# Sums of squares of k, q and the outputs made in parts, inside a two-layer decoder trunk

## The chip, the core and the metric

The kernel runs on one core of a Trainium2 chip, in one launch. The metric is the device time of one execution in microseconds (us); lower is better. TensorE is PE below (its weight loads PEld), VectorE is DVE, ScalarE is ACT, GpSimd is POOL, and SyncE, which issues most weight loads, is SP.

## What is computed

A causal decoder trunk of two layers for 512 tokens of width 1024, in float32. Each layer is a mixer, a cross attention into 256 memory tokens and a gated convolutional feed-forward net. The change lies in the mixer of layer 0, and there in its gated delta rule: 4 heads of 128, with k and q normalised to length 1 and the output normalised again per head.

```python
qkv = silu(causal_dwconv(qkv, conv_qkv))
q, k, v = heads(qkv)                       # 4 heads x 128
q, k = l2_normalize(q), l2_normalize(k)    # x * rsqrt(sum(x * x) + 1e-6)
beta, g = sigmoid(b), -exp(a_log) * softplus(a + dt_bias)
o = gated_delta_rule_chunked(q, k, v, g, beta)     # q is scaled by 128 ** -0.5 inside
o = rms_norm(o, onorm_g) * silu(gate)
y_b = glu(gelu(s5_ssm(u)))                 # a diagonal state-space model beside it
x = x + concat(o, y_b) @ w_out
```

So three sums of squares are needed for each token and head: of k, of q, and of the output o.

## The kernel before

Activations lie transposed: 128 features on the partitions, 512 tokens along the free dimension. A float32 product is made of three matmuls (`mm3`, L182 to L187), with each operand split into a rounded part (`wh`, `xh`) and a rest (`wl`, `xl`). Weights come by DMA into three `raw` tiles; ACT rounds them (`wh`, L136) and DVE subtracts (`wl`, L141), for some of them POOL adds the rest by an accumulating DMA (L139). A sum over the 128 features of a head is a matmul of a tile of squares with a column of ones: `sumsq` (L764) makes one column for each head and chunk of 128 tokens, 4 per tile, each of them two records in the trace.

The mixer is a list of steps, `MIX`, at the head of the file. It is the order in which the program is written. PE and SP run in exactly that order; DVE, ACT and POOL run in an order that a scheduler makes when the program is built, so a change to one step can move other instructions on them.

The steps that matter here:

- `k`, `kc`, `qp` project k and q, convolve them (`cv`, L753 to L756), and square them on ACT (L761). `ba` makes beta and the decay g; its exponential and logarithm (L690 to L722) work on DVE in columns of `area`, a PSUM tile of 1024 columns that `column` (L107) hands out slice by slice.
- `ssk` (L863) is k's sums: 16 columns into a PSUM tile called `tr`, one of a ring of six (`psum`, L116), then 1 / sqrt on DVE (`rsqrt`, L197, some ten short instructions L204 to L211).
- `gc`, `rg`, `eg`, `rk` sum g up and lay the factors out as rows: `rows3` (L283) splits 32 columns into three parts on DVE (`R`, L290 to L293), transposes them on PE (L295), and ACT rounds the result (`RT`, L297). `dec` then multiplies them out into rows on PE (`row`, L305 and L307).
- `su` (`ssm_u`, L1377) brings u of the state-space model into another layout through DRAM: DVE scales (`sp`, L1383), ACT's queue stores (`du`, L1385) and loads it in four parts (`su`, L1388).
- `qk` (L934) makes the masked scores and q's sums; `B` is one piece of the memory's keys (`kp`) and values (`vp`), used to fill PE; `xa`, `xb` (`xstage`, L1011) and `ya`, `yb` (`ystage`) are steps of the inverse of a triangular matrix.
- `cs` updates the state, `co` (L1072) makes the outputs of one chunk in PSUM (`po`) and copies them into `oT` on ACT; `so` (L1085) squares the four `oT`, sums them in 16 columns, and makes from q's and the output's sums the factor `ro`, which `rr` and `yo` use.

The memory's norm (`r`, made by the same `rsqrt`) is laid out as rows by `row` (L262) for `B`.

Of the kernel before, what the change touches and what calls it, by code (L numbers as in the profile page):

```python
# [21 lines left out]
D = 1024  # L22
# [6 lines left out]
EPS = 1e-6  # L29
# [16 lines left out]
k3 k0 ba rs k1 rb kc1 bt su0 k2 kc2 su3 kc3 kc0 qp3 ssk sw0 gc su1 vp1 rg eg rk dec0 dec1 kh1 sw1 vp3 dec3 kh2 st0  # L46
dec2 am1 kh0 su2 am2 am0 kh3 sc0 vt3 am3 i i i i vp0 i st1 vp2 i i i i i i i sc1 sy0 gp1 i i gp3 i i i i sw2 qp1 vt1 i
gp2 qp2 i i qp0 i vt2 gp0 i i i i i sy1 ea0 i i i ea1 i i qk1 st2 ea2 i qk0 eb2 i i i ea3 mem kt2 qk3 qk2 B ya0 ya1
sc2 eb3 eb1 ya2 eb0 ya3 B sw3 B xa0 xa1 xa3 vt0 yb0 B xa2 yb2 B kt0 xb0 yb3 xb2 kt1 B W2 yb1 sy2 U2 B U0 B xb3 W0 xb1
kt3 U3 U1 W1 cs0 co0 W3 B cw1 B cs1 B B B co1 B B B cw2 st3 cs2 cw3 sc3 B co2 co3 B so B ld sy3 B B rr B B B B gu0 yo2  # L50
B gu1 B B yo0 B yo1 B yo3 B B gu2 gu3
# [5 lines left out]
class Net:  # L57
# [49 lines left out]
    def column(self, n, s="y"):  # L107

        if self.area is None:
            return self.tiny(n, s)  # L110
        if self.cur + n > 1024:
            self.cur = 0
        self.cur += n
        return self.area[:, self.cur - n : self.cur]
# [649 lines left out]
    def sumsq(self, squares):  # L764

        ps = self.psum("tr")
        for h, sq in enumerate(squares):
            for c in range(4):
                self.nc.tensor.matmul(ps[:, h * 4 + c : h * 4 + c + 1], sq[:, c * 128 : (c + 1) * 128], self.ones[:, 0:1], start=True, stop=True)  # L769
        return ps[:, : 4 * len(squares)]  # L770

    def mixer0(self, N, kv_out, x):
# [26 lines left out]
        g, ro = mp(16, "g"), mp(16, "ro")  # L799
# [62 lines left out]

        def ssk():  # L863
            va = self.tiny(16, "ssk")
            v.tensor_scalar(va, self.sumsq(sqk), EPS, None, ALU.add)
            self.rsqrt(va, 16, out=rkG[:, 0:16])
# [67 lines left out]
        def qk(h):  # L934
            ps = self.psum("qk")
            for c in range(4):
                nc.tensor.matmul(ps[:, CS[c]], kT[h][:, CS[c]], qT[h][:, CS[c]], start=True, stop=True)
            a = decT[h]
            v.tensor_tensor(a, ps, a, ALU.mult)
            QK[h] = a  # L940
            sq = ssq[:, 4 * h : 4 * h + 4]
            v.tensor_scalar(sq, self.sumsq([sqq[h]]), EPS, None, ALU.add)
            ps = self.rowr(D["Rk"], range(16 + 4 * h, 20 + 4 * h))
            v.tensor_tensor(qT[h], qT[h], ps, ALU.mult)
# [199 lines left out]
        def ld():  # L1144
# [5 lines left out]
            k=k, kc=kc, rs=rs, rb=rb, ba=ba_, bt=bt_, vp=vp, gp=gp, qp=qp, ssk=ssk, gc=gc, rg=rg, eg=eg, rk=rk, dec=dec, kh=khat, am=amat,  # L1150
# [440 lines left out]
```

## Time and profile before

| | us |
|---|---|
| median of 3 runs (lowest to highest) | 1418.5 (1417.56 to 1419.75) |
| the profiled execution | 1423.21 |
| its span, first to last instruction | 1421.2 |
| PE busy in the span | 1362.0 |
| DVE, ACT, POOL busy in the span | 915.4, 623.5, 222.6 |
| mean granted clock of TensorE | 0.970 of full |

The span is that of the profiled execution, whose own time is 2.0 us longer than its span and 4.7 us longer than the median. An engine's busy time says how much it has to do; what bounds the kernel at a place is read from the idle time of the engine that is busy nearly always, PE, and from what ended that idle time. A granted clock of 1 stands for 2.4 GHz and of 0.5 for 1.2 GHz.

### The profile page before, as it was taken

The numbers are of one execution on the slowest core, as the hardware profiler recorded it, in microseconds if no ns is written. First come the engines' busy times: TensorE is split into PE (matmuls) and PEld (weight loads), VectorE is DVE, ScalarE is ACT, GpSimd is POOL, SyncE is SP. The second block draws the span as 40 slices with busy tenths as digits, with TensorE's granted clock in tenths as the row PEclk, the third lists the DMA queues.
The fourth block names the chain that finished last, engine by engine and source line by source line (L and its number), as shares of the span: only waits on it lengthen the run. The fifth ranks groups of instructions, "written<-read, shape, count | busy, mean of one in ns | idle before, by whom it ended". The sixth has DMA issues, their size and how long they took to land.

```text
span 1421.2 us, 17648 instructions
## 1 busy us (share of the span) xinstructions
PE 1362.0 (96%) x6699; PEld 1150.6 (81%) x6699; DVE 915.4 (64%) x1551; ACT 623.5 (44%) x951; POOL 222.6 (16%) x351
## 2 busy tenths in 40 slices
PE   8599987999999999999999999989999999999997
PEld 6578876987788888888888888768888888888886
DVE  7867968457655567637754765975657746763764
ACT  6347564545434444314432445554444413431442
POOL 2594826220200200000000002210110000000003
PEclk9779968999999999999999999999999999999998
DMA  7343524375331233233333235942233333323221
GB/s 226 101 99 80 149 48 109 87 189 140 104 89 46 87 91 95 84 113 95 104 89 104 90 97 153 227 116 59 65 100 96 97 100 94 103 75 119 86 68 69
DMA packets 50772, 147.16 MB, mean 104 GB/s; under 512 B 7680, under 2 KB 13952, under 8 KB 50688
## 3 DMA queue, kind: packets, MB, share of 16 engines
q1 hardware_dynamic: 40480, 127.29, 29.4%
q0 software_dynamic: 3888, 14.16, 5.8%
q10 hardware_dynamic: 6320, 4.60, 1.1%
q8 instruction: 52, 0.85, 0.2%
q14 instruction: 32, 0.26, 0.1%
HBM read 141.83 MB, written 4.19 MB: 103 GB/s over the span
## 4 chain that ended last, share of the span: by engine, by line
PE 79%; DMA 3%; DVE 2%; ACT 2%; issue 1%; POOL 1%; ACTq 0%; POOLq 0%; SPq 0%
PE in L185 13%; PE in L187 13%; PE in L186 13%; PE op L186 9%; PE op L185 9%; PE op L187 9%; DMA raw<-in_wk 1%; PE kp L187 1%; PE kp L186 1%; PE kp L185 1%; DMA wl<-in_wk 1%; PE tr L769 1%; PE vp L185 1%; PE vp L186 1%; PE sc L187 1%
## 5 line engine op out<-in xcount | busy, mean ns | idle before, releaser
L136 ACT CAST wh<-raw 128x1024 fp32r<-128x1024 f32 (+1 forms) x230 | 237.4, 1036 | 397.6 <-PE op L186 152.0
L185 PE MATMUL in<-xh,wh 128*128 128x512 f32 x992 | 392.0, 395 | 13.2 <-DVE vl L374 6.3
L186 PE MATMUL in<-xl,wh 128*128 128x512 f32 x992 | 389.7, 393 | 0.0
L187 PE MATMUL in<-xh,wl 128*128 128x512 f32 x992 | 389.0, 392 | 0.0
L141 DVE TENSOR_TENSOR wl<-raw,wh 128x1024 fp32r<-128x1024 f32 (+1 forms) x203 | 244.1, 1205 | 79.4 <-ACT wh L136 77.1
L185 PEld LDWEIGHTS in<-xh,wh 128*128 128x128 f32 x992 | 188.5, 190 | 52.3 <-DVE vl L374 6.5
L187 PEld LDWEIGHTS in<-xh,wl 128*128 128x128 f32 x992 | 188.3, 190 | 39.6
L186 PEld LDWEIGHTS in<-xl,wh 128*128 128x128 f32 x992 | 188.4, 190 | 39.2 <-DVE xl L227 0.9
L247 POOL TENSOR_TENSOR sq<-sq,sq 128x512 f32<-128x512 f32 x28 | 47.5, 1698 | 973.2 <-ACT sq L242 875.2
L469 DVE TENSOR_TENSOR x<-op,x 128x512 f32<-128x512 f32 x68 | 46.9, 691 | 151.7 <-PE op L187 151.7
L185 PE MATMUL op<-fh,wh 128*128 128x512 f32 (+1 forms) x376 | 141.4, 376 | 0.0
L187 PE MATMUL op<-fh,wl 128*128 128x512 f32 (+1 forms) x376 | 141.2, 375 | 0.0
L186 PE MATMUL op<-fl,wh 128*128 128x512 f32 (+1 forms) x376 | 141.2, 375 | 0.0
L572 DVE TENSOR_TENSOR h<-in,rB 128x512 f32<-128x512 f32 x88 | 60.2, 688 | 87.1 <-PE in L187 87.1
L186 PEld LDWEIGHTS op<-fl,wh 128*128 128x128 f32 x376 | 70.8, 188 | 12.8
L185 PEld LDWEIGHTS op<-fh,wh 128*128 128x128 f32 x376 | 70.8, 188 | 12.8
L187 PEld LDWEIGHTS op<-fh,wl 128*128 128x128 f32 x376 | 70.8, 188 | 12.8
L192 ACT CAST fh<-a 128x512 fp32r<-128x512 f32 x44 | 27.3, 621 | 110.6 <-DVE a L584 110.6
L576 ACT ACTIVATE a<-h,small 128x512 f32<-128x512 f32 x88 | 63.3, 721 | 10.5 <-DVE h L572 9.8
L578 DVE SCALAR_TENSOR_TENSOR a<-h,small,a 128x510 f32<-128x510 f32 x88 | 65.8, 749 | 2.9
L577 DVE SCALAR_TENSOR_TENSOR a<-h,small,a 128x511 f32<-128x511 f32 x88 | 65.5, 746 | 2.5 <-ACT a L576 2.5
L580 ACT ACTIVATE a<-a 128x512 f32<-128x512 f32 x44 | 27.8, 632 | 81.0 <-DVE a L578 80.9
(459 smaller groups left out, 2137.1 us busy)
## 6 DMA issues: line engine op xcount, KB each, us to landing
raw<-in_up SPq DMA_DIRECT2D x88, 512.0 KB, 3.6
raw<-in_dn SPq DMA_DIRECT2D x32, 512.0 KB, 3.7
raw<-in_w_in SPq DMA_DIRECT2D x18, 512.0 KB, 4.5
raw<-in_wk SPq DMA_DIRECT2D x16, 512.0 KB, 4.6
raw<-in_wv SPq DMA_DIRECT2D x16, 512.0 KB, 4.0
raw<-in_wq SPq DMA_DIRECT2D x16, 512.0 KB, 4.2
raw<-in_wo SPq DMA_DIRECT2D x16, 512.0 KB, 3.7
raw<-in_dn SPq DMA_DIRECT2D x16, 384.0 KB, 3.0
```

The source lines that it names most:

```text
L136: nc.scalar.copy(H, raw)
L141: nc.vector.tensor_tensor(L, raw, H.bitcast(F32), ALU.subtract)
L185: mm(ps, wh, xh, start=start, stop=False)
L186: mm(ps, wh, xl, start=False, stop=False)
L187: mm(ps, wl, xh, start=False, stop=stop)
L247: eng.tensor_tensor(N["acc"], N["acc"], sq, ALU.add)
L469: nc.vector.tensor_tensor(x[m], ps, x[m], ALU.add)
L572: nc.vector.tensor_tensor(h, ps, rB, ALU.mult)
L576: nc.scalar.activation(a, h, AF.Copy, scale=cw(2))
L577: nc.vector.scalar_tensor_tensor(a[:, 1:], h[:, : T - 1], cw(1), a[:, 1:], ALU.mult, ALU.add)
L578: nc.vector.scalar_tensor_tensor(a[:, 2:], h[:, : T - 2], cw(0), a[:, 2:], ALU.mult, ALU.add)
L580: nc.scalar.activation(a, a, AF.Silu)
```

## The change

1. `sumsq` sums one tile of squares into columns that the caller gives.
2. k's sums become steps of their own, `sk0` to `sk3`, placed right before `ssk`. They write the last 16 columns of `area`, which `column` no longer hands out; `ssk` reads them there. A `tr` tile of the ring is saved.
3. `qk` takes its `tr` tile itself; its work is the same.
4. `co` squares its chunk of outputs on ACT straight from PSUM, before the copies into `oT`. The sums of a chunk are made at the start of the next `co`, those of the last one in `so`, in a new PSUM tile `sso` of 16 columns, ordered by chunk and then head.
5. 1 / sqrt of q's sums and its square over 128 (`cq`, `c2`) are computed at the first `co` and no longer in `so`.

```diff
-k3 k0 ba rs k1 rb kc1 bt su0 k2 kc2 su3 kc3 kc0 qp3 ssk sw0 gc su1 vp1 rg eg rk dec0 dec1 kh1 sw1 vp3 dec3 kh2 st0
+k3 k0 ba rs k1 rb kc1 bt su0 k2 kc2 su3 kc3 kc0 qp3 sk0 sk1 sk2 sk3 ssk sw0 gc su1 vp1 rg eg rk dec0 dec1 kh1 sw1 vp3
...
-        if self.cur + n > 1024:
+        if self.cur + n > 1008:
...
-    def sumsq(self, squares):
-
-        ps = self.psum("tr")
-        for h, sq in enumerate(squares):
-            for c in range(4):
-                self.nc.tensor.matmul(ps[:, h * 4 + c : h * 4 + c + 1], sq[:, c * 128 : (c + 1) * 128], self.ones[:, 0:1], start=True, stop=True)
-        return ps[:, : 4 * len(squares)]
+    def sumsq(self, sq, out):
+
+        for c in range(sq.shape[1] // 128):
+            self.nc.tensor.matmul(out[:, c : c + 1], sq[:, c * 128 : (c + 1) * 128], self.ones[:, 0:1], start=True, stop=True)
...
+        def sk(h):
+            self.sumsq(sqk[h], self.area[:, 1008 + 4 * h : 1012 + 4 * h])
+
         def ssk():
             va = self.tiny(16, "ssk")
-            v.tensor_scalar(va, self.sumsq(sqk), EPS, None, ALU.add)
+            v.tensor_scalar(va, self.area[:, 1008:1024], EPS, None, ALU.add)
             self.rsqrt(va, 16, out=rkG[:, 0:16])
...
+        def sums():
+            for c in list(sqo):
+                self.sumsq(sqo.pop(c), D["sso"][:, 4 * c : 4 * c + 4])
+
         def co(c):
+            if "sso" not in D:
+
+                D["sso"] = self.px.tile([128, 16], F32, tag="px", name="sso")
+                c_ = D["c"] = self.rsqrt(ssq, 16, out=mp(16, "cq"))
+                v.tensor_scalar_mul(c_, c_, 128.0 ** -0.5)
+                v.tensor_mul(c2, c_, c_)
+                v.tensor_scalar_mul(c2, c2, 1.0 / 128)
+            sums()
             po = self.psum("o")
...
+            sqo[c] = self.square(po)
             for h in range(4):
-                if c == 0:
+                if oT[h] is None:
                     oT[h] = self.t(F32, "oT")
                 nc.scalar.copy(oT[h][:, CS[c]], po[:, CS[h]])
...
         def so():
             assert all(D["o", c] for c in range(4))
-            sso = self.sumsq([self.square(o) for o in oT])
-            c_ = self.rsqrt(ssq, 16)
-            v.tensor_scalar_mul(c_, c_, 128.0 ** -0.5)
+            sums()
             m2 = self.tiny(16, "m2")
-            v.tensor_mul(m2, c_, c_)
-            v.tensor_tensor(m2, m2, sso, ALU.mult)
-            v.tensor_scalar(m2, m2, 1.0 / 128, EPS, ALU.mult, ALU.add)
+            hc = lambda t: t.rearrange("p (h c) -> p h c", c=4)
+            v.tensor_tensor(hc(m2), hc(c2), D["sso"].rearrange("p (c h) -> p h c", h=4), ALU.mult)
+            v.tensor_scalar(m2, m2, EPS, None, ALU.add)
             self.rsqrt(m2, 16, out=ro)
-            v.tensor_mul(ro, ro, c_)
+            v.tensor_mul(ro, ro, D["c"])
             D["ro"] = ro
```

What the change does to the order of the instructions is shown at three places. Line numbers of the changed kernel differ by a few.

**PE, k's sums.** Here PE comes from the projection of q's head 3, sums the squares of k (`sq`), multiplies g with a triangle and with ones (`G`), and goes on to the projection `in`. Before:

```order
L769 MATMUL tr_851<-ones,sq_807 128x1 [waits DVE_49,PE_49,Activation_49]
L769 MATMUL tr_851<-ones,sq_807 128x1 x3
L769 MATMUL tr_851<-ones,sq_610 128x1 x4
L769 MATMUL tr_851<-ones,sq_749 128x1 x4
L769 MATMUL tr_851<-ones,sq_798 128x1 x4
L870 MATMUL G_930<-g,triu 128x16 [waits DVE_49,Pool_49]
```

Changed:

```order
L767 MATMUL area<-ones,sq_808 128x1 [waits DVE_49,Activation_49]
L767 MATMUL area<-ones,sq_808 128x1 x3
L767 MATMUL area<-ones,sq_611 128x1 x4
L767 MATMUL area<-ones,sq_750 128x1 x4
L767 MATMUL area<-ones,sq_799 128x1 x4
L871 MATMUL G_930<-g,triu 128x16 [waits DVE_49,PE_49,Pool_49]
```

The sums stand at the same place in PE's order; they write `area` where they wrote a `tr` tile. Both wait for DVE and ACT. The signal of DVE that they wait for is its 86th before, and its 198th in the changed program; the 198th is that of `g<-z,area` (L847), the last instruction of `ba` that reads `area`.

**DVE, the factors and u.** Between the exponential of the decays (`eG`) and the next projection, DVE makes the parts `R` of the factors `rkG` and scales u (`sp`, of step `su1`). Before:

```order
L950 MEMSET X_1425 128x1024
L883 COPY rkG<-eG_245 128x16 [waits DVE_49]
L884 COPY sKb<-eG_245 128x16
L885 TENSOR_TENSOR sK<-beta,eG_245 128x16
L1383 TENSOR_TENSOR sp_970<-in_945,rB_601 128x512 [waits PE_49]
L951 MEMSET X_1425 128x32 [waits DVE_49]
L290 CAST R_170_1050<-rkG 128x32 [waits DVE_49]
L291 TENSOR_TENSOR r_171_1052<-rkG,R_170_1050 128x32 [waits DVE_49]
L292 CAST R_170_1050<-r_171_1052 128x32 [waits DVE_49]
L293 TENSOR_TENSOR R_170_1050<-r_171_1052,R_170_1050 128x32 [waits DVE_49]
```

Changed:

```order
L953 MEMSET X_1425 128x1024
L884 COPY rkG<-eG_245 128x16 [waits DVE_49]
L885 COPY sKb<-eG_245 128x16
L886 TENSOR_TENSOR sK<-beta,eG_245 128x16
L954 MEMSET X_1425 128x32 [waits DVE_49]
L290 CAST R_169_1050<-rkG 128x32 [waits DVE_49]
L291 TENSOR_TENSOR r_170_1052<-rkG,R_169_1050 128x32 [waits DVE_49]
L292 CAST R_169_1050<-r_170_1052 128x32 [waits DVE_49]
L293 TENSOR_TENSOR R_169_1050<-r_170_1052,R_169_1050 128x32 [waits DVE_49]
L1397 TENSOR_TENSOR sp_970<-in_945,rB_602 128x512 [waits PE_49]
```

`sp` went from ahead of the five instructions on `X` and `R` to behind them.

**DVE, the memory's norm.** In the inverse, DVE subtracts products from the blocks `X` (L1019, L1020), finishes the memory's `r` (L208 to L211) and makes two `wl` of the keys' weights. Before:

```order
L211 SCALAR_TENSOR_TENSOR r_2361<-rsq_2363,r_2361 128x2 [waits DVE_49]
L208 TENSOR_TENSOR rst_2362<-r_2361 128x2 [waits DVE_49]
L141 TENSOR_TENSOR wl_2557<-raw_2554,wh_2556 128x1024 [waits DMAHW1_49,DMASW0_49,Activation_49]
L209 TENSOR_TENSOR rsu_2364<-rst_2362,rsv_2365 128x2 [waits DVE_49]
L210 SCALAR_TENSOR_TENSOR rsq_2363<-rsu_2364 128x2 [waits DVE_49]
L211 SCALAR_TENSOR_TENSOR r_2361<-rsq_2363,r_2361 128x2 [waits DVE_49]
L141 TENSOR_TENSOR wl_2690<-raw_2687,wh_2689 128x1024 [waits DMASW1_49,DMAHW2_49,PE_49,Activation_49]
L1019 TENSOR_TENSOR X_2132<-X_2132,Xl_2540 128x512 [waits PE_49]
```

Changed:

```order
L208 TENSOR_TENSOR rst_2362<-r_2361 128x2 [waits DVE_49]
L209 TENSOR_TENSOR rsu_2364<-rst_2362,rsv_2365 128x2 [waits DVE_49]
L210 SCALAR_TENSOR_TENSOR rsq_2363<-rsu_2364 128x2 [waits DVE_49]
L1022 TENSOR_TENSOR X_2144<-X_2144,Xl_2486 128x512 [waits PE_49]
L1023 TENSOR_TENSOR X_2150<-X_2150,Xu_2481 128x512
L211 SCALAR_TENSOR_TENSOR r_2361<-rsq_2363,r_2361 128x2 [waits DVE_49]
L141 TENSOR_TENSOR wl_2557<-raw_2554,wh_2556 128x1024 [waits DMAHW1_49,DMASW0_49,Activation_49]
L141 TENSOR_TENSOR wl_2690<-raw_2687,wh_2689 128x1024 [waits DMASW1_49,DMAHW2_49,PE_49,Activation_49]
L1022 TENSOR_TENSOR X_2132<-X_2132,Xl_2540 128x512 [waits PE_49]
```

The last instruction of the norm, `r` (L211), went from between the two `wl` to ahead of both.

## Rows read from the trace of the kernel before

**Rows 1.** The page, part 1: busy us (share of the span) xinstructions.

```profile
PE 1362.0 (96%) x6699; PEld 1150.6 (81%) x6699; DVE 915.4 (64%) x1551; ACT 623.5 (44%) x951; POOL 222.6 (16%) x351
```

**Rows 2.** Timeline, PE, 51 to 95: start us, us, ..., [idle before <-releaser].

```profile
66.24 6.99 PE L769 MATMUL tr<-ones,sq 128*128 128x1 f32 x32 [14.54 <-ACT sq L761]
...
90.49 0.33 PE L305 MATMUL row<-RT,sel 128*128 128x128 f32 x1 [2.55 <-ACT RT L297]
...
92.51 1.91 PE L305 MATMUL row<-RT,sel 128*128 128x128 f32 x8
94.22 0.73 PE L185 MATMUL in<-xh,wh 128*128 128x512 f32 x1
```

**Rows 3.** Timeline, ACT, 64 to 93 us.

```profile
83.79 0.34 ACTq L1385 DMA_DIRECT2D du<-sp  x1
88.32 1.81 ACTq L1388 DMA_DIRECT2D su<-du  x4
90.17 0.43 ACT L297 CAST RT<-R 128x128 fp32r<-128x128 f32 x2 [15.88 <-issue]
```

**Rows 4.** Timeline, DVE, 64 to 93 us.

```profile
70.11 0.17 DVE L847 SCALAR_TENSOR_TENSOR g<-z,area 128x16 f32<-128x16 f32 x1
...
73.27 0.18 DVE L865 TENSOR_SCALAR ssk<-tr 128x16 f32<-128x16 f32 x1 [0.96 <-PE tr L769]
...
82.69 1.06 DVE L1383 TENSOR_TENSOR sp<-in,rB 128x512 f32<-128x512 f32 x1
...
86.28 1.22 DVE L293 TENSOR_TENSOR R<-r,R 128x32 fp32r<-128x32 f32 x1
```

**Rows 5.** One line's instructions, L1385: its last row.

```profile
DMA to landing us min/median/max: 2.0/3.3/6.2
```

**Rows 6.** Stretches: us, PE PEld DVE ACT POOL busy (x), PEclk, DMA, GB/s.

```profile
95.00:100.00 5.00, 5.00 (x15) 3.89 (x15) 1.28 (x2) 4.96 (x7) 4.78 (x7) 0.61 0.00 0
180.00:185.00 5.00, 5.00 (x45) 4.92 (x45) 4.00 (x13) 3.37 (x5) 3.05 (x6) 1.00 0.63 85
```

**Rows 7.** Timeline, PE, 226 to 250 us.

```profile
229.46 1.16 PE L1014 MATMUL Xu<-X,Y 128*128 128x128 f32 x8 [1.78 <-ACT Y L1008]
...
233.65 1.13 PE L1006 MATMUL Y<-X,E 128*128 128x128 f32 x8
...
240.40 0.66 PE L267 MATMUL row<-ident,r 128*128 128x128 f32 x2 [4.21 <-DVE r L211]
...
242.56 1.91 PE L1018 MATMUL Xl<-Y,X 128*128 128x128 f32 x8
245.34 2.05 PE L1006 MATMUL Y<-X,E 128*128 128x128 f32 x8 [0.87 <-DVE X L1019]
```

**Rows 8.** Timeline, DVE, 233 to 250 us.

```profile
237.72 1.22 DVE L141 TENSOR_TENSOR wl<-raw,wh 128x1024 fp32r<-128x1024 f32 x1 [1.93 <-ACT wh L136]
...
239.78 0.47 DVE L211 SCALAR_TENSOR_TENSOR r<-rsq,r 128x2 f32<-128x2 f32 x1
240.18 1.21 DVE L141 TENSOR_TENSOR wl<-raw,wh 128x1024 fp32r<-128x1024 f32 x1
244.51 0.69 DVE L1019 TENSOR_TENSOR X<-X,Xl 128x512 f32<-128x512 f32 x1 [3.12 <-PE Xl L1018]
```

**Rows 9.** Timeline, ACT, 233 to 250 us.

```profile
236.65 1.04 ACT L136 CAST wh<-raw 128x1024 fp32r<-128x1024 f32 x1 [1.50 <-DMA raw<-in_wk]
...
238.61 1.06 ACT L136 CAST wh<-raw 128x1024 fp32r<-128x1024 f32 x1
```

**Rows 10.** Timeline, PE, 296 to 326 us.

```profile
303.33 3.73 PE L769 MATMUL tr<-ones,sq 128*128 128x1 f32 x32
```

**Rows 11.** Stretches at the end of the mixer, columns as in rows 6.

```profile
305.00:310.00 5.00, 5.00 (x28) 4.42 (x28) 4.20 (x14) 0.45 (x1) 1.66 (x2) 0.72 1.02 383
310.00:315.00 5.00, 5.00 (x34) 4.54 (x33) 2.21 (x7) 1.94 (x3) 0.20 (x3) 0.94 0.49 143
```

**Rows 12.** Timeline, ACT, 296 to 326 us.

```profile
302.61 2.22 ACT L761 ACTIVATE sq<-oT 128x512 f32<-128x512 f32 x4
```

More of the change, by code (lines that the diff above doesn't have):

```diff
@@ L45 @@
 MIX = """
-k3 k0 ba rs k1 rb kc1 bt su0 k2 kc2 su3 kc3 kc0 qp3 ssk sw0 gc su1 vp1 rg eg rk dec0 dec1 kh1 sw1 vp3 dec3 kh2 st0
[L47 to L51, printed above, removed]
+k3 k0 ba rs k1 rb kc1 bt su0 k2 kc2 su3 kc3 kc0 qp3 sk0 sk1 sk2 sk3 ssk sw0 gc su1 vp1 rg eg rk dec0 dec1 kh1 sw1 vp3
+dec3 kh2 st0 dec2 am1 kh0 su2 am2 am0 kh3 sc0 vt3 am3 i i i i vp0 i st1 vp2 i i i i i i i sc1 sy0 gp1 i i gp3 i i i i
+sw2 qp1 vt1 i gp2 qp2 i i qp0 i vt2 gp0 i i i i i sy1 ea0 i i i ea1 i i qk1 st2 ea2 i qk0 eb2 i i i ea3 mem kt2 qk3
+qk2 B ya0 ya1 sc2 eb3 eb1 ya2 eb0 ya3 B sw3 B xa0 xa1 xa3 vt0 yb0 B xa2 yb2 B kt0 xb0 yb3 xb2 kt1 B W2 yb1 sy2 U2 B U0
+B xb3 W0 xb1 kt3 U3 U1 W1 cs0 co0 W3 B cw1 B cs1 B B B co1 B B B cw2 st3 cs2 cw3 sc3 B co2 co3 B so B ld sy3 B B rr B
+B B B gu0 yo2 B gu1 B B yo0 B yo1 B yo3 B B gu2 gu3
 """.split()
@@ L798, in mixer0 @@
         sK, sKb, ssq = mp(16, "sK"), mp(16, "sKb"), mp(16, "ssq")
-        g, ro = mp(16, "g"), mp(16, "ro")
+        g, ro, c2 = mp(16, "g"), mp(16, "ro"), mp(16, "c2")
+        sqo = {}
         G, eG, eGL = G3[:, 0:16], eG3[:, 0:16], eG3[:, 32:48]
@@ L941, in qk @@
             sq = ssq[:, 4 * h : 4 * h + 4]
-            v.tensor_scalar(sq, self.sumsq([sqq[h]]), EPS, None, ALU.add)
+            pq = self.psum("tr")
+            self.sumsq(sqq[h], pq)
+            v.tensor_scalar(sq, pq[:, 0:4], EPS, None, ALU.add)
             ps = self.rowr(D["Rk"], range(16 + 4 * h, 20 + 4 * h))
@@ L1149, in mixer0 @@
         do = dict(
-            k=k, kc=kc, rs=rs, rb=rb, ba=ba_, bt=bt_, vp=vp, gp=gp, qp=qp, ssk=ssk, gc=gc, rg=rg, eg=eg, rk=rk, dec=dec, kh=khat, am=amat,
+            k=k, kc=kc, rs=rs, rb=rb, ba=ba_, bt=bt_, vp=vp, gp=gp, qp=qp, ssk=ssk, sk=sk, gc=gc, rg=rg, eg=eg, rk=rk, dec=dec, kh=khat, am=amat,
             vt=vtr, kt=ktok, qk=qk, i=i, ea=e0, eb=e1, ya=y0, xa=x0, yb=y1, xb=x1, U=lambda h: uw(U, h, Xu[h], vT[h], "U"), W=lambda h: uw(WT, h, Kbg[h], Xu[h], "W"),
```

## The prediction

> **What bounds the kernel now.** I read the busy times first. PE works 1362.0 us [rows 1] of a span of 1421.2 us, so nearly everything else hides behind it, and the change removes no PE work: 48 small matmuls stay 48. What it can move is the rest, some 60 us in which PE is idle, and the stretches at half clock behind such idle time. So I went through PE's timeline at the places the change touches, then through ACT's and DVE's for what ended each wait, then through the order of the changed program for what stands elsewhere. Three places count.
>
> At the front PE waits 14.54 us for the square of k's head 0, then makes the 32 records of k's sums at half clock in 6.99 us, and after the next projection it waits 2.55 us for `RT` [rows 2]. That `RT` is late because of ACT's own queue: the store `du` starts at 83.79, the load `su` behind it only at 88.32, and `RT` stands behind both [rows 3]. In the middle PE waits 4.21 us for the memory's `r`, and, soon after, 0.87 us for `X` [rows 7]. At the end 32 records of the outputs' sums stand in one burst of 3.73 us [rows 10], after which the granted clock sinks to 0.72 and 0.94 of full [rows 11].
>
> From 95 to 185 us PE is busy 5.00 of 5 us in all 18 stretches (the first and the last stand in [rows 6]). Time lost ahead of it is therefore not made up there; the waits behind it end on DVE and ACT work that starts from PE's results, and shift along.
>
> **Front: k's sums wait longer.** Before, their first matmul starts when the square is done, at 66.24 [rows 2]. In the changed program it waits for the signal of `g<-z,area`, since the sums now lie in the tile that this instruction reads. It runs from 70.11 for 0.17 [rows 4] and ends at 70.28. With about 0.14 for the signal the sums start at 70.42: **+4.18 us**. Behind the sums stand G, the projection, and on DVE `ssk`, which waited 0.96 us for the sums already [rows 4], so it shifts too. POOL's work isn't delayed, and covers nothing here.
>
> **Front: `sp` behind `R`.** In the order of the change, `sp` stands behind the split of `rkG`. Before, it ran 82.69 to 83.75, and the split after it until 87.50 (86.28 + 1.22) [rows 4]. Without `sp` in front, the split would start 1.0 us earlier and, 4.2 later by the wait, end near 90.5; `sp` then ends near 91.5. `du` goes out at 91.55. In this kernel `du` takes 2.0 us at least, 3.3 in the median and 6.2 at most to land [rows 5]; here it was 4.5 (83.79 to 88.32 [rows 3]), with weight loads in the air. I take 2.1, since the accumulating load next to it will be through by then. So `su` is issued at 93.65, takes 1.81, `RT` starts at 95.5 (90.17 before [rows 3]), and PE's rows at 95.8 instead of 90.49: +5.3, that is **+1.1** on top of 4.18. Were `du` to land in 3.3 us it is +2.3 and in 6.2 it is +5.2; were the split quicker than before by 1 us, +0.1.
>
> PE has then been idle for some 4.4 us instead of 2.55. Before, the clock fell only in the middle of the 24 rows: the last 8 take 1.71 us to the next projection (92.51 to 94.22), 0.214 each, the first 16 just 2.02 us [rows 2]. After the longer gap I take all 24 at 0.214: 5.1 us for 3.73, **+1.4**. Bounds: 0 if the clock holds as long as before, 2.0 if the projection behind runs longer at half clock. Sum of the front: **+6.7**, between +4.2 and +10.8.
>
> **Middle: `r` is early.** `r` (239.78 + 0.47) ended PE's wait at 240.40. It stood behind one `wl`, ahead of which DVE was idle for 1.93 us waiting for ACT [rows 7, 8]. In the changed order the last three short instructions of `r` stand ahead of it and fit into that idle time, so PE's `row` can start near 236.4. What is late next is `X`: it now stands behind both `wl`, and the second needs ACT's second `wh`, 238.61 + 1.06 = 239.67 [rows 9]. 239.67 + 1.21 for `wl` + 0.69 for `X` [rows 8] gives 241.6, so `Y` starts at 241.7 and not at 245.34: **-3.6**. The `wl` could not come sooner, as ACT's first `wh` waited for its DMA for 1.50 us [rows 9]. Two other subtractions of `X` come some tenths later behind q's factors, which now stand there; I take +0.3 and thus **-3.3**.
>
> The clock may add to this. Before, PE ran this stretch at half clock: 8 matmuls of `Y` took 2.05, against 1.13 a little earlier [rows 7]. In the changed order PE would have two gaps, a short one near 236.2 and, after 18 matmuls, one of about 2.8 us before `Y`. A gap of 1.78 us kept the clock (8 matmuls in 1.16 behind it) [rows 7], one of 2.55 lost it soon after [rows 2], so I let it fall again. The Trainium skill, "TensorE: Matmul & The Clock Gate", section "Why this matters for your kernels", warns only of longer idle gaps between bursts, and by it this one might pass at full clock; the 2.55 us gap speaks against that. If the clock holds, some 3.7 us of work behind `Y` that ran at half clock take 1.9 less: -5.5 in all by rows 7. At worst, with the second `wl` late by a further 2 us, the middle gives -1.
>
> **End: four parts for one burst.** The 32 records cost 3.73 us in one piece [rows 10] and as much in four eights. What can be saved is the dip in the clock behind the burst: (1 - 0.72) x 5 + (1 - 0.94) x 5 = 1.7 us [rows 11]. Against that, the sums of chunk 2 now stand between `co2` and `co3` on PE and wait for ACT's square of chunk 2. One square takes some 0.63 us (four take 2.22 [rows 12]); with signals PE stalls **+0.8**. The last eight are covered by the `B` behind `co3`. Net **-0.9**; if the clock dips anyway, +0.9, and if the stall hides, -1.7.
>
> **Priced at nothing.** q's factors leave `so` for the first `co`: some ten DVE instructions of 0.17, hidden by PE, and `ro` isn't needed before `rr`; uncovered, 2 us. `co0`'s square delays the copy behind it on ACT by 0.63, just covered by the state step behind it; uncovered, up to 0.6. The last load of x waits for one DVE scan more on SP, with weights queued behind it, whose users come some 7 us later. The ring of six PSUM tiles turns by one `tr` less; no wait of PE hangs on it that I found, 0.5 either way.
>
> **Sum.** +6.7 - 3.3 - 0.9 = **+2.5 us** on the profiled execution's 1423.2, that is 1425.7. That execution stands 4.7 us above the median, so the forecast is 1418.5 + 2.5 = **1421.0 us**, still within what a measurement of this kernel can hardly tell from no change (0.2%, 2.8 us: 1415.7 to 1421.3).
>
> **Rivals.**
>
> 1. *u comes back late (slower).* As above, but `du` meets the weight load in flight and takes 6.2 us, the highest [rows 5]. `RT` is on ACT behind `su`, so each microsecond beyond 2.1 goes to PE in full: +4.1, **1425.1**. It decides as soon as `su` is issued later than about 93.7. For it: the same store took 4.5 last time. Against: from 95 to 100 us no transfer ran at all [rows 6]. Chance 0.14.
> 2. *The middle gives nothing (slower).* `row` starts early but `Y` waits for `X` behind two late `wl` as long as now, because ACT's second `wh` gets its data later. Then 6.7 - 0.9 = +5.8, **1424.3**. For it: the DMA is what ACT waited for there [rows 9]. Chance 0.10.
> 3. *The clock pays (faster).* The clock holds in the middle (-5.5) and the end gains its 1.7, while at the front only the wait of 4.18 counts, as the split runs faster in its new place and the rows keep their clock: 4.2 - 5.5 - 1.7 = -3.0, **1415.5**. For it: the 1.78 us gap. Against: three favourable things. Chance 0.18.
> 4. *The wait is not there.* If DVE is ahead of its times before at the front, and `g` is done when the square is, the front costs 0 to 2.5, and the sum is -4.2 to -1.7: **1414.3 to 1416.8**. Against: DVE's timeline has no idle time ahead of `g`, and 4 us of work would have to go. Chance 0.10.
> 5. *Nothing moves on the path:* 1418.5, chance 0.06.
>
> **How the numbers follow.** The forecast has the chance 0.42, with its own range of 1419 to 1423; I give 0.30 of it to "same" and 0.12 to "slower". Rivals 1 and 2 are slower (0.24). Rival 3 is faster with 0.14 and same with 0.04, rival 4 0.06 and 0.04, rival 5 0.02 and 0.04. Faster 0.22, same 0.42, slower 0.36. The range 1415.0 to 1425.5 takes in rivals 1, 2, 3 and half of 4.
>
> **What would show it.** On PE, k's sums start near 70.4 behind a wait that ends on DVE; rows L305 start near 95.8, and at 100 us PE is 6 to 7 us behind. In the middle the wait of 4.21 for `r` is gone and one of some 3 us for `X` stands before `Y`. At the end four groups of eight sums, one behind a wait of 0.8 for ACT, and a clock near 1.0 from 305 on. I am wrong if k's sums start by 67, if `du` lands after more than 4 us, if the wait for `r` remains, or if an idle time of PE over 2 us appears where none is named here.

## The result: 1.1% slower, and the profile after

The changed kernel takes 1434.88 us in the median of 4 runs (1429.86 to 1441.7), the kernel before 1419.12 on the same chip. The ratio is 1.0113 [1.0083, 1.0142]. That is slower by over five times the 0.2% that the prediction takes for no difference, and outside its range. A second set of runs, told below, gave 1.0070 [1.0046, 1.0094]: the loss is 10 to 16 us.

The profiled execution took 1441.7 us, its span is 1439.8. PE is busy 7.0 us longer than before [rows 1], at as many matmuls, so the rest of the 18.6 us by which the span grew is idle time:

```profile
PE 1369.0 (95%) x6699; PEld 1156.1 (80%) x6699; DVE 921.9 (64%) x1552; ACT 622.9 (43%) x951; POOL 220.6 (15%) x351
```

The waits of PE at the places of the change, from the timeline of PE in the profile after:

```profile
71.87 6.96 PE L767 MATMUL area<-ones,sq 128*128 128x1 f32 x32 [18.77 <-DVE g L845]
...
97.87 0.48 PE L305 MATMUL row<-RT,sel 128*128 128x128 f32 x1 [4.80 <-ACT RT L297]
...
118.40 0.47 PE L305 MATMUL row<-RT,sel 128*128 128x128 f32 x1 [1.68 <-DVE kb L904]
...
246.31 1.16 PE L1017 MATMUL Xu<-X,Y 128*128 128x128 f32 x8 [1.75 <-DVE X L1022]
...
252.08 0.40 PE L267 MATMUL row<-ident,r 128*128 128x128 f32 x2 [0.30 <-DVE r L211]
...
255.48 1.13 PE L1009 MATMUL Y<-X,E 128*128 128x128 f32 x8 [1.21 <-DVE X L1022]
...
278.11 1.51 PE L1044 MATMUL U<-cv,X 128*128 128x128 f32 x8 [2.02 <-DVE X L1023]
...
314.25 1.05 PE L767 MATMUL sso<-ones,sq 128*128 128x1 f32 x8 [0.69 <-ACT sq L761]
...
336.27 0.50 PE L185 MATMUL glu<-glh,wh 128*128 128x512 f32 x1 [2.13 <-ACT glh L192]
```

The first, second, fifth, sixth and eighth are those that the prediction named, [rows 2] and [rows 7] before. The fourth is one of the two other subtractions of `X`, which it priced at 0.3. The third, the seventh and the ninth, on `kb`, on `U` and on `glh`, it did not name; the one on `U` needs no change, as is shown below. How late each piece of PE's work is against the trace before (start there, start here, difference) says what each place cost:

| PE's work | before | after | later by |
|---|---|---|---|
| k's sums | 66.24 | 71.87 | 5.6, of which 1.4 from the start of the program |
| rows L305 behind `RT` | 90.49 | 97.87 | 7.4 |
| projection behind them | 94.22 | 103.05 | 8.8 |
| rows of the next head | 107.61 | 118.40 | 10.8 |
| projection behind them | 110.34 | 123.59 | 13.2 |
| `row` of the memory's `r` | 240.40 | 252.08 | 11.7 |
| the memory's keys behind `Y` | 248.90 | 257.39 | 8.5 |
| state step ahead of the first outputs' sums | 276.40 | 288.03 | 11.6 |
| behind the outputs' sums | 310.64 | 321.40 | 10.8 |
| first `glu` | 323.50 | 336.27 | 12.8 |
| a later `glu` | 328.15 | 343.79 | 15.6 |
| end of the span | 1421.2 | 1439.8 | 18.6 |

The 1.4 us at the start is the clock, which came up later in this execution; in the second profile of the same program it isn't there. The last 3 us come in the second layer, at a load of weights, and in that second profile they are gone too. What lies between is the front (7.4 us up to the first projection, 11.8 up to the second), the middle (from 13.1 us late at 242 to 8.5 at 257), the wait for `U` (from 8.5 to 11.6, with the half clock behind it) and the end.

The granted clock of the stretches that matter (PE's busy time first, then the clock third from the right; the columns are those of [rows 6]):

```profile
115.00:120.00 5.00, 3.32 (x23) 2.71 (x22) 4.93 (x5) 1.01 (x2) 1.66 (x2) 0.83 0.96 211
120.00:125.00 5.00, 5.00 (x22) 4.71 (x22) 2.64 (x4) 4.46 (x10) 0.00 (x0) 0.50 0.44 174
125.00:130.00 5.00, 5.00 (x24) 4.14 (x23) 0.00 (x0) 2.21 (x4) 0.00 (x0) 0.98 0.00 0
...
250.00:255.00 5.00, 3.97 (x34) 3.60 (x32) 4.99 (x7) 2.46 (x6) 4.80 (x5) 1.00 0.65 162
255.00:260.00 5.00, 4.52 (x40) 4.55 (x41) 4.51 (x8) 1.94 (x5) 4.77 (x7) 1.00 0.77 257
...
320.00:325.00 5.00, 5.00 (x35) 4.56 (x34) 3.26 (x19) 0.98 (x2) 0.20 (x3) 1.00 0.60 225
335.00:340.00 5.00, 3.14 (x9) 2.53 (x10) 2.38 (x3) 3.55 (x5) 0.00 (x0) 0.68 0.86 192
340.00:345.00 5.00, 5.00 (x16) 3.89 (x15) 3.63 (x5) 2.22 (x3) 0.00 (x0) 0.64 0.01 2
```

Behind the waits for `kb` and `glh` the clock goes to half. In the middle, which ran at half clock before, it stays at full. The dip behind the burst of outputs' sums [rows 11] is gone (320 to 325 is the place), but in its stead there is one 15 us later.

**Who made `kb` late.** DVE's timeline, and POOL's beside it:

```profile
113.55 4.21 DVE L141 TENSOR_TENSOR wl<-raw,wh 128x1024 fp32r<-128x1024 f32 x1
117.67 0.67 DVE L904 TENSOR_TENSOR kb<-cv,row 128x512 f32<-128x512 f32 x1
```

```profile
113.22 0.92 POOL L139 DMA_DIRECT2D wl<-in_w_in  x1 [5.39 <-ACT wl L138]
113.89 1.55 POOL L1358 TENSOR_TENSOR ct<-ct,tt 128x512 f32<-128x512 f32 x1
115.12 1.54 POOL L1362 TENSOR_TENSOR st<-st,tt 128x512 f32<-128x512 f32 x1
```

A `wl` stands right ahead of `kb` and takes 4.21 us, where it takes 1.22 elsewhere [rows 8]; it ends 1.1 us after POOL's `st`. In the trace before, DVE makes no `wl` between 104 and 113 us. The scheduler put it there.

**Who made `glh` late.** ACT's timeline after (`dy` stores the outputs of the state-space model, `so` loads them in another layout, `glh` rounds them for `glu`):

```profile
324.24 0.34 ACTq L1457 DMA_DIRECT2D dy<-sg  x1
...
327.91 1.05 ACT L136 CAST wh<-raw 128x1024 fp32r<-128x1024 f32 x1 [0.18 <-PE vp L187]
327.99 1.81 ACTq L1460 DMA_DIRECT2D so<-dy  x4
...
335.15 1.07 ACT L192 CAST glh<-so 128x512 fp32r<-128x512 f32 x1 [2.33 <-DMA so<-dy]
```

and before:

```profile
313.48 0.34 ACTq L1443 DMA_DIRECT2D dy<-sg  x1
...
316.86 1.76 ACTq L1446 DMA_DIRECT2D so<-dy  x4
...
322.33 1.12 ACT L192 CAST glh<-so 128x512 fp32r<-128x512 f32 x1 [0.56 <-DMA so<-dy]
```

Before, one `wh` stood between `dy` and `so`; now there are three, and the third starts only at 327.91, when the second is through and PE has freed its buffer, with `so` behind it. `dy` lands in 2.0 us now, where it took 3.4 before, yet `so` is issued no sooner: 3.75 us behind `dy`, 3.38 before. Then `so` itself lands in 5.2 us in the median instead of 4.2, with weight loads in the air, and from `so` to `glh` it is 7.16 us instead of 5.47. So `glh` comes 2.1 us later relative to `dy`.

### The profile page after: what moved, and what is told of

Same layout as the page of the kernel before. It is cut to its first block, busy times and chain, and to the rows that moved or that the text cites. A ratio compares the mean times of both kernels' runs of the same rounds, so it can differ in the third digit from the quotient of the medians.

```text
span 1439.8 us, 17647 instructions
## 1 busy us (share of the span) xinstructions
PE 1369.0 (95%) x6699; PEld 1156.1 (80%) x6699; DVE 921.9 (64%) x1552; ACT 622.9 (43%) x951; POOL 220.6 (15%) x351
## 4 chain that ended last, share of the span: by engine, by line
PE 78%; DVE 3%; DMA 2%; ACT 2%; issue 1%; POOL 0%; ACTq 0%; POOLq 0%; DVEq 0%
PE in L185 13%; PE in L187 13%; PE in L186 13%; PE op L185 8%; PE op L186 8%; PE op L187 8%; DMA wl<-in_wk 1%; PE kp L187 1%; PE kp L186 1%; PE kp L185 1%; PE vp L185 1%; PE vp L186 1%; PE vp L187 1%; DMA so<-dy 1%; PE sc L187 1%
## 5 line engine op out<-in xcount | busy, mean ns | idle before, releaser
L141 DVE TENSOR_TENSOR wl<-raw,wh 128x1024 fp32r<-128x1024 f32 (+1 forms) x203 | 248.1, 1226 | 73.9 <-ACT wh L136 71.6
L186 PEld LDWEIGHTS op<-fl,wh 128*128 128x128 f32 x376 | 70.8, 188 | 12.8
L187 PEld LDWEIGHTS op<-fh,wl 128*128 128x128 f32 x376 | 70.8, 188 | 12.8
```

Of the source, the lines that this page charges most:

```text
L141: nc.vector.tensor_tensor(L, raw, H.bitcast(F32), ALU.subtract)
L186: mm(ps, wh, xl, start=False, stop=False)
L187: mm(ps, wl, xh, start=False, stop=stop)
```

## The experiments

Three sets of runs were made, each with the kernel before beside it on the same chip: 1421.34, 1420.85 and 1420.38 us in the median. Two theories stood against each other for the loss: that it is all the place of k's sums in `area` (with what follows at the front), or that the outputs' part, `co` and `so`, costs time of its own by the order it gives ACT. Several edits use a helper that the kernel has, `behind(ins, gate)` (L86): the scheduler then places `ins` after `gate` on its engine, and nothing waits on the chip for it.

### Both kernels again, unchanged

> The changed kernel once more, for a second profile. Theory A (the wait on area and the orders of DVE that come with it make the loss): k's sums start some 4.2 us later than before again, counted from the same start of PE's full clock; the row matmuls about 7.4 later, and behind the split of the second kb 11 to 12 later; the middle gives 3 to 5 back. Theory B (the loss is mostly chance of where DMAs fall): these shifts differ from the first profile by several us. The 1.4 us at the very start and the 3.7 us in the second layer of the first profile (waits for clock and DMA that the change does not touch) should not come again in both theories. Time 1428 to 1440.

> The kernel before, unchanged, for a second profile and as a measure of what two identical programs differ by: 1419 to 1423, ratio 0.998 to 1.002. If the store dy in the middle (issued near 260 us) again takes 2.4 us until the load so is issued, the 4 us that the other kernels show there belong to the change; if it takes about 4 us, the first profile of before was the lucky one, and PE's wait of 1.4 to 1.6 us for X before the second U is no cost of the change. The half clock from 188 to 215 us should show the same here if it belongs to the kernel.

The changed kernel: 1433.29 us (1424.48 to 1436.13, 8 runs), ratio 1.0070 [1.0046, 1.0094]. The kernel before: 1420.01, against itself 0.9990 [0.9972, 1.0007]. So the loss is there again, and single executions of either kernel differ by some 10 us. The profile of this run of the changed kernel is its quickest execution and shows which parts of the loss are steady. The wait of 18.80 for `g`, that of 4.83 for `RT` and that of 2.12 for `glh` are there; the wait for `kb` isn't, so that PE is 7.35 us late at the second projection (117.69) and not the 11 to 12 that were expected. The order on DVE is the same, but here POOL came just behind the `wl`:

```profile
111.84 1.22 DVE L141 TENSOR_TENSOR wl<-raw,wh 128x1024 fp32r<-128x1024 f32 x1
112.98 0.68 DVE L904 TENSOR_TENSOR kb<-cv,row 128x512 f32<-128x512 f32 x1
```

```profile
111.89 0.92 POOL L139 DMA_DIRECT2D wl<-in_w_in  x1 [5.39 <-ACT wl L138]
112.56 1.64 POOL L1358 TENSOR_TENSOR ct<-ct,tt 128x512 f32<-128x512 f32 x1
```

The second profile of the kernel before takes one suspect away. PE's wait for `U`, 2.02 us after the change, is 1.83 us there, since the store `dy` of an earlier step took 4.5 us to land and ACT's queue stood behind it:

```profile
254.79 0.34 ACTq L1443 DMA_DIRECT2D dy<-sg  x1
259.26 1.76 ACTq L1446 DMA_DIRECT2D so<-dy  x4
```

In the first profile of before the same two rows lie 2.37 us apart. In all 14 profiles the wait for `U` goes with this store: none where `dy` took 2.2 to 2.4 us to land, 0.86 to 2.02 where it took 3.2 to 4.5. The wait for `U` therefore needs no change to come. Whether the change makes it more frequent is open: the long landing is in 10 of the 11 profiles of kernels with the change or a part of it, and in 1 of the 3 of the kernel before, with or without the order of `r` told below.

### The two halves of the change

`r3_area_alone` is the kernel before with k's sums in the columns of `area`, and nothing else:

```diff
-        if self.cur + n > 1024:
+        if self.cur + n > 1008:
...
-    def sumsq(self, squares):
+    def sumsq(self, squares, ps=None):
...
-        ps = self.psum("tr")
+        ps = self.psum("tr") if ps is None else ps
...
-            v.tensor_scalar(va, self.sumsq(sqk), EPS, None, ALU.add)
+            v.tensor_scalar(va, self.sumsq(sqk, self.area[:, 1008:1024]), EPS, None, ALU.add)
```

> The kernel before with one edit: k's sums in the last 16 columns of area. Theory A: nearly the whole loss, 1428 to 1436, with the wait for g, for RT, and for kb at the front, r early in the middle. Rival B (co and so make the loss): 1420 to 1424.

`r2_own_tile` is the changed kernel with k's sums in a `tr` tile of their own again:

```diff
-            self.sumsq(sqk[h], self.area[:, 1008 + 4 * h : 1012 + 4 * h])
+            if "pk" not in D:
+                D["pk"] = self.psum("tr")
+            self.sumsq(sqk[h], D["pk"][:, 4 * h : 4 * h + 4])
...
-            v.tensor_scalar(va, self.area[:, 1008:1024], EPS, None, ALU.add)
+            v.tensor_scalar(va, D["pk"][:, 0:16], EPS, None, ALU.add)
```

> The change with k's sums in a tr tile of the ring instead of columns of area; the parts on co, so and the factors of q stay. Theory A: the wait at k's sums is as before (sums start when the square of k's head 0 is done), the orders of DVE at the front and in the middle are those of before, and the time falls by 11 to 16 us to 1417 to 1421. Rival B (the parts in co and so cost as much, by round trips through DRAM that land later): 1424 to 1430, with the wait for glh of about 2 us at the end still there.

The columns alone: 1427.24 us, 1.0054 [1.0038, 1.0070]. The rest alone: 1424.89 us, 1.0023 [1.0004, 1.0042]. Both halves lose, and their sum, 0.77%, agrees with the 0.70% of the whole; the 1.13% of the first runs lies higher. The first theory, that nothing but the columns costs time, had put `r2_own_tile` at 1417 to 1421 and fails; `r3_area_alone` lies between what the two theories had for it.

The wait at k's sums is there with the columns,

```profile
71.39 6.96 PE L769 MATMUL area<-ones,sq 128*128 128x1 f32 x32 [19.48 <-DVE g L847]
...
97.21 0.47 PE L305 MATMUL row<-RT,sel 128*128 128x128 f32 x1 [4.84 <-ACT RT L297]
...
117.26 0.33 PE L305 MATMUL row<-RT,sel 128*128 128x128 f32 x1 [1.68 <-DVE kb L903]
```

and gone with the own tile, where the square ends it as before [rows 2], while the wait for `glh` stays:

```profile
66.50 6.99 PE L767 MATMUL tr<-ones,sq 128*128 128x1 f32 x32 [14.87 <-ACT sq L761]
...
326.19 0.50 PE L185 MATMUL glu<-glh,wh 128*128 128x512 f32 x1 [2.09 <-ACT glh L192]
```

So `g`, `RT` and `kb` belong to the columns and `glh` belongs to `co` and `so`. The columns also carry the gain in the middle: the kernel with the columns alone waits 0.29 us for the memory's `r`, that with the own tile 3.60. The order on DVE at 240 us thus hangs on where 16 columns lie at 70 us.

### The order of `sp` at the front

`r9_sp_first` is the changed kernel with the first split of `rkG` behind `sp`, as it stood before the change:

```diff
-    def rows3(self, r, n):
+    def rows3(self, r, n, gate=None):
...
-        v.tensor_copy(part(0).bitcast(F32R), r)
+        ins = v.tensor_copy(part(0).bitcast(F32R), r)
+        if gate is not None:
+            self.behind(ins, gate)
...
-            D["Rk"] = self.rows3(rkG, 32)
+            D["Rk"] = self.rows3(rkG, 32, self.sp)
...
-        nc.vector.tensor_tensor(A, q4(ps), q4(rB), ALU.mult)
+        self.sp = nc.vector.tensor_tensor(A, q4(ps), q4(rB), ALU.mult)
```

> The changed kernel with one order forced on DVE: sp of step su1 ahead of the split R of rkG, as in the kernel before. Forecast's term: RT comes 1.1 to 2.3 us earlier, so PE's rows L305 start 5.2 to 5.6 us later than before (with the same start of k's sums as in the changed kernel) and not 6.6 to 7; 1 to 2 us less than the changed kernel. Rival: du lands later in its new place, no gain.

1429.74 us, 1.0067 [1.0040, 1.0093]. The rows L305 start behind a wait of 1.60 instead of 4.80:

```profile
94.11 0.33 PE L307 MATMUL row<-RT,sel 128*128 128x128 f32 x1 [1.60 <-ACT RT L299]
```

From the start of the sums to the rows it is 23.3 us, against 26.0 in the first profile of the changed kernel and 26.6 in the second, and the first rows now take 0.28 each and not 0.41, so that the projection behind them stands 27.1 us behind the sums and not 31.2 and 31.8. The order of `sp` is shown as the cause of this wait, and its price at the place is 2.7 to 3.3 us up to the rows and 4.1 to 4.7 up to the projection; the medians (4 runs here) don't tell the gain apart, and in this profile the wait for `kb` was there.

### `kb` ahead of the second `wl`

```diff
-            nc.vector.tensor_tensor(L, raw, H.bitcast(F32), ALU.subtract)
+            ins = nc.vector.tensor_tensor(L, raw, H.bitcast(F32), ALU.subtract)
+            if self.gate is not None:
+                self.behind(ins, self.gate)
+                self.gate = None
...
-            v.tensor_tensor(Kb[h], kT[h], ps, ALU.mult)
+            kb = v.tensor_tensor(Kb[h], kT[h], ps, ALU.mult)
+            if h == 2:
+                self.gate = kb
```

> The changed kernel with one order forced on DVE: the second wl at the front stands behind kb of head 2. Theory A: PE's wait of 1.68 us for kb at about 118 us is gone, and with it the half clock behind it (2.3 us): 3 to 4.5 us less than the changed kernel on the same chip. Rival (the clock falls there anyway, or the wl then delays what comes next): 0 to 1 us less.

1432.13 us (4 runs), 1.0076 [1.0048, 1.0103]. The wait for `kb` is gone and the `wl` takes 1.22, yet no gain shows: against the unchanged order the median is 1432.13 for 1433.29, the ratio 1.0076 for 1.0070. The profile lost its time elsewhere: from 204 to 212 us it ran at clock 0.50, where the second profile of the changed kernel had 0.96 and 1.00, and between 193 and 220 us it falls back by 4.6 us against it. What `kb` is worth in the median stays open.

### The memory's `r` ahead of both `wl`

The kernel before, with the first `wl` behind the last instruction of `r`:

```diff
-            nc.vector.tensor_tensor(L, raw, H.bitcast(F32), ALU.subtract)
+            ins = nc.vector.tensor_tensor(L, raw, H.bitcast(F32), ALU.subtract)
+            if self.rgate is not None:
+                self.behind(ins, self.rgate)
+                self.rgate = None
...
-            i.scalar_tensor_tensor(y, q, 1.875, y, ALU.add, ALU.mult)
+            ins = i.scalar_tensor_tensor(y, q, 1.875, y, ALU.add, ALU.mult)
+        if n == 2:
+            self.rgate = ins
```

> The kernel before with one order forced on DVE: the last three instructions of the memory's r ahead of the first of the two wl, as the change has them. By the forecast's term for the middle PE's wait of 4.21 us for r goes, one of about 1 us for X stays, and the time falls by 3.3 us (clock lost again) to 5.5 us (clock held). Rival: X is late by as much, 0 to 1 us less.

1417.11 us, 0.9970 [0.9950, 0.9989]: faster by 4.3 us, the middle of the changed kernel by itself.

```profile
237.37 0.41 PE L273 MATMUL row<-ident,r 128*128 128x128 f32 x2 [1.16 <-DVE r L215]
...
240.68 1.16 PE L1012 MATMUL Y<-X,E 128*128 128x128 f32 x8 [1.12 <-DVE X L1025]
```

Against [rows 7] `row` starts 3.0 us earlier and `Y` 4.7, and the 8 matmuls of `Y` take 1.16 instead of 2.05: the clock held. A theory that the wait for `X` takes the place of that for `r` would have left `Y` where it was.

### `so` ahead of the third `wh` at the end

In the version with the own tile (`r7_own_tile_so`) and in the changed kernel itself (`r10_so_first`), the third `wh` after the last `dy` and all later ones go behind `so` on ACT:

```diff
-        nc.scalar.copy(H, raw)
+        ins = nc.scalar.copy(H, raw)
+        if self.agate is not None:
+            self.skip -= 1
+            if self.skip < 0:
+                self.behind(ins, self.agate)
...
-            nc.scalar.dma_start(o[j * 32 : j * 32 + 32], d[:, j, :].rearrange("(t c) n -> c t n", t=4))
+            ins = nc.scalar.dma_start(o[j * 32 : j * 32 + 32], d[:, j, :].rearrange("(t c) n -> c t n", t=4))
+        if ut == 3:
+            self.agate, self.skip = ins, 2
```

> The kernel of r2_own_tile (k's sums in a tr tile, parts on co and so kept) with one order forced on ACT: at the end the third wh stands behind the loads so, as in the kernel before. Theory A (the wait of 2.1 us for glh at the end comes from ACT's order: the freed ACT casts weights ahead of so, the buffers it frees are refilled while so is in flight): the wait falls below 1 us, the half clock behind it goes, and the time is 3 to 4 us below r2_own_tile. Rival (dy and so are slow for other reasons): no change against r2_own_tile.

> The changed kernel with one order forced on ACT: at the end the third wh behind the loads so. As on the kernel with the own tile, where it took 5 us off: the wait of 2.1 us for glh and the half clock behind it go, 4 to 5 us less than the changed kernel (1428 to 1430). Rival: the gain there was a chance of that phase, 0 to 1 us.

With the own tile 1419.63 us, 0.9990 [0.9972, 1.0009], after 1.0023 without the order: the ratio falls by 0.0033, some 4.7 us (1 to 8 by the two intervals). In the changed kernel 1427.52 us, 1.0057 [1.0039, 1.0075], lower than 1.0070 and 1.0113 but with an interval that overlaps the first of these. In both, PE's wait for `glh` is gone. ACT's timeline of the version without the order, and of that with it:

```profile
314.17 0.34 ACTq L1459 DMA_DIRECT2D dy<-sg  x1
...
317.94 1.80 ACTq L1462 DMA_DIRECT2D so<-dy  x4
...
325.06 1.07 ACT L192 CAST glh<-so 128x512 fp32r<-128x512 f32 x1 [1.73 <-DMA so<-dy]
```

```profile
307.70 0.34 ACTq L1464 DMA_DIRECT2D dy<-sg  x1
...
310.43 1.41 ACTq L1467 DMA_DIRECT2D so<-dy  x3
...
316.51 1.10 ACT L197 CAST glh<-so 128x512 fp32r<-128x512 f32 x1
```

From `dy` to `glh` 8.8 us instead of 10.9, and the clock of the ordered version is 1.00 from 300 to 335. So the loss of the half `co` and `so` is the order on ACT, not the sums in parts.

### All three orders in the changed kernel

`r12_orders_mended` is the changed kernel with the three edits on `sp`, `kb` and `so` together.

> The changed kernel with all three orders forced: sp ahead of R, kb ahead of the second wl, and the third wh behind so. What is left of the change is the wait on area (4.2 us), the longer half clock behind it (1 to 1.5), the early r (4 to 5 back) and the sums in parts (1 to 2 back). If this is the whole account, the time comes to 1419 to 1424, within 0.3% of the kernel before; if the wait on area costs more by another way, above 1426.

1424.1 us, 1.0028 [1.0011, 1.0046], at the upper edge of what was expected. No wait for `kb` or `glh`, 1.87 for `RT`. Of the 0.70% of the second set of runs 0.42 is mended. Against `r10_so_first`, in the same set, the orders of `sp` and `kb` together give 0.0029, some 4 us (1 to 8 by the two intervals).

What remains, some 4 us (1.6 to 6.5), is more than the known terms give. The wait for `g` is still there (18.82 us at the sums, 4.2 more than before), but so are the early `r`, which gives back 4.3 by itself, and the sums in parts, which give back 0.9 in the traces. By these three the kernel should be 1 us faster than the kernel before. In its profile PE also waits 1.64 us for `U`; whether that is a part of the rest, and what else is, isn't shown.

### A version better than both

The own tile, with `r` ahead of both `wl` and `so` ahead of the third `wh`; and the same with the sums of a chunk behind the next chunk's matmuls, so that PE needn't wait for the square:

```diff
-            sums()
             po = self.psum("o")
...
+            sums()
             sqo[c] = self.square(po)
```

> Both forced orders on the kernel of r2_own_tile: r ahead of the two wl on DVE, and the third wh behind the loads so on ACT. If both theories hold, 3 to 5 us below the kernel before: ratio 0.996 to 0.998. If neither, like r2_own_tile (1.002).

> r8_best with the sums of a chunk's outputs behind the next chunk's output matmuls and not ahead of them. PE's wait of 0.69 us for ACT's square between co2 and co3 goes: 0.5 to 1 us below r8_best, ratio to the kernel before 0.996 to 0.997. Rival: the square delays the copies on ACT instead, no change.

1415.87 us, 0.9970 [0.9953, 0.9986], and 1415.13 us, 0.9966 [0.9953, 0.9980]. Both are 4 to 5 us quicker than the kernel before. The stall of 0.69 is gone in the second; between the two no difference can be measured. The kernel before with the order of `r` alone has the same 0.9970, so no gain of the sums in parts over that is shown.

## Why the prediction was wrong

**Front, the wait: right.** Forecast +4.18. The sums start 18.77 to 18.80 us after PE's last work instead of 14.54, +4.2, and `g` ends the wait. With a tile of its own the wait is gone.

**Front, `sp` behind `R`: right in kind, too small.** `du` landed in 2.04 us (93.67 to 95.71), for 2.1 assumed:

```profile
93.67 0.34 ACTq L1399 DMA_DIRECT2D du<-sp  x1
95.71 1.80 ACTq L1402 DMA_DIRECT2D su<-du  x4
97.55 0.27 ACT L297 CAST RT<-R 128x128 fp32r<-128x128 f32 x1 [21.82 <-issue]
```

Rows L305 are 1.75 us later than the wait alone explains (7.38 - 5.63), in the second profile 2.35 (97.10 - 90.49 - 4.26), for 1.1. Most of the difference is the split: it ends 5.16 us later than before (92.66 for 87.50) where the sums start 5.63 later, so without `sp` ahead of it it gained 0.5 us and not 1.0. (By the prediction's own terms it would end at 87.50 - 1.0 + 4.2 = 90.7, not near 90.5.) All 24 rows ran at half clock, +1.4, as forecast. Up to the projection the front cost 7.4 us (8.8 less the 1.4 of the start), within the bounds of 4.2 to 10.8 (whose upper end is 11.4 by its own terms) and near the 6.7. Rival 1, a late `du`, did not come.

**Front, behind 95 us: the first miss.** The prediction took DVE's work behind this to "start from PE's results, and shift along", and read DVE's order only to 93 us. A few rows on, the new order has a `wl` right ahead of `kb`. In the profiled execution PE waits 1.68 us there and runs at half clock behind it, and between the two projections it falls back by 4.4 us (8.8 to 13.2). It was there in 4 of the 7 profiles of kernels with the columns in `area`, counting the two in which `kb` was put first. Behind it the clock fell in two of the four, where PE falls back by 4.4 and 4.3 us between the projections (the change and `r9_sp_first`), and held in two, where it falls back by 1.5 and 1.6 (`r3_area_alone` and `r10_so_first`). The medians don't settle its share.

**Middle: right in kind, too small.** Forecast -3.3, with -5.5 if the clock holds (-5.2 with its own 0.3). It held: PE is 13.1 us late at 242 and 8.5 at 257, a gain of 4.6, and with the order alone the kernel before gains 4.3 (0.0030 [0.0011, 0.0050] of 1420). The terms came out otherwise than forecast, though. The other two subtractions of `X`, behind q's factors, cost not 0.3 but 2.4 (PE waits 1.75 us for one of them and is 15.4 late at 248). Then the wait for `r` gives back 3.7 and the full clock another 3.2. The wait for `X` ahead of `Y` is 1.21 us and not some 3, since PE came to it later. The prediction weighed here what the Trainium skill, "TensorE: Matmul & The Clock Gate", section "Why this matters for your kernels", says of longer gaps alone. At this place the trace agrees with it: the clock was kept over the 1.21 us. Elsewhere the traces don't: the 2.13 us before `glu` lost it, and the 1.68 before `kb` lost it in two profiles and kept it in two.

**End, the parts: right.** The stall before the sums of chunk 2 is 0.69 us, for 0.8, and the clock's dip is gone, for 1.7 us. The net was forecast at -0.9. From the state step at 288 us, ahead of the first eight sums, to 321 PE goes from 11.6 us late to 10.8: a gain of 0.9 with all 32 records and the stall paid, and 0.85 to 0.89 in all nine profiles with the sums at these places.

**End, "Priced at nothing": the step that failed.** The squares leave `so`, where ACT worked 2.22 us on them [rows 12]. The prediction costed ACT's new squares, but it never asked how the scheduler would order ACT's other work without the old ones, and so put nothing for that. Of the last four `wh` ahead of `glh`, one stood ahead of `dy` before, one between `dy` and the load `so`, and two behind `so`. In the new order three stand between `dy` and `so`; why the scheduler chose it isn't shown. So `glh` came late, PE waited 2.13 us and ran at half clock behind it. In the profile this is 15.64 - 10.76 = 4.9 us from 321 to 344, in the medians 4.7 us. That it is the order, `r7_own_tile_so` and `r10_so_first` show: with the third `wh` behind `so` the wait is gone. With it, the end costs 4.9 - 0.9 = 4.0 where -0.9 was forecast. The prediction's own sign of being wrong came here, an idle time of PE over 2 us where none was named.

**The sum.** In the profile the terms are 4.2 for the wait, 3.2 for `RT` and its half clock (8.8 - 5.6), 4.4 for `kb`, 4.9 at `glh`, less 4.6 in the middle and 0.9 for the parts: 11.2 us, or 6.8 in an execution without the wait for `kb`. The second set of runs has 9.9 us (0.70%), the first 15.8.

By the halves the outputs' part loses 0.23% or 3.3 us where -0.9 was forecast, and the 4.7 at `glh` are that difference. The columns lose 0.54% or 7.7 us where 6.7 - 3.3 = 3.4 was forecast. Of the 4.3 us that are missing there `RT` is 0.65, and `kb` 1.5 to 4.4 where it comes, while the middle gave 1.0 more than forecast. That these orders are all of it isn't shown, since 4 us remain with all three mended. The kernel's own spread of some 10 us between executions, of which three runs before had shown 2, is why the range should have been wider too.

## What to carry to other kernels

Where a scheduler orders the engines, work taken off an engine is a change to the order there: look at how its other work is ordered now, and whether a transfer that someone waits for has come to stand behind more of it. Follow the new order on each engine until the old one is back, not only at the lines of the diff. Columns of a tile that other steps use bring their waits with them: 16 columns saved a ring tile and cost 4.2 us at once.

## What the runs showed of the hardware

**`wl` beside POOL.** The subtraction of 128 x 1024 right ahead of `kb` took 1.22 us or 4.21 in the five profiles with this order. In all four profiles with 4.21 (starting at 113.55, 112.39, 108.21 and 113.02) POOL had started its DMA issue 0.3 us ahead of it, and `ct` and `st` of POOL ran through before `wl` ended, 1.1 us after `st`. Where `wl` started 0.05 us ahead of POOL (111.84 against 111.89) it took 1.22. So in these five profiles the time goes with who started first. At other places beside POOL's work the same subtraction took values between, 1.80 for one at 108.06 in `r12_orders_mended`. The Trainium skill, "SBUF — State Buffer", section "SBUF: two separate sides", says that VectorE with two inputs there and a GpSimd instruction that reads there share a pair of ports, which whoever starts first holds for its whole instruction. The traces agree if POOL's DMA issue is counted as such an instruction, which this section does not say, and show that here DVE did not get its turn between POOL's `ct` and `st` either.

**A store and its reload.** From the store `dy` to the load `so` behind it, the same place of the program took 2.2 to 4.5 us, in the kernel before (2.37 and 4.47) as in the variants. In the second profile of the kernel before little moves at the end: 4 GB/s from 257 to 258 us and 17 from there to 258.6, with `so` issued at 259.26. Why is open.

**When the clock comes back.** The same program can lose some us here. The granted clock from 204 to 208 us, in the first and in the second profile of the kernel before:

```profile
204.00:208.00 4.00, 4.00 (x20) 4.00 (x20) 1.61 (x5) 3.03 (x9) 0.00 (x0) 0.50 0.00 0
```

```profile
204.00:208.00 4.00, 4.00 (x31) 4.00 (x32) 3.49 (x12) 3.72 (x11) 0.00 (x0) 0.82 0.00 0
```

PE is busy all 4 us in both; it fell to half in both at the same wait, near 188 us. What makes it return earlier in one isn't shown.
